# A hybrid decoder layer on one core: the stage of gates, w_out and routing turns its rows by VectorE from quarters of columns instead of by TensorE

## The chip, the core and the metric

The kernel runs on one core of a Trainium2 chip. A core has TensorE (PE: matrix products; PEld is its weight load), VectorE (DVE), ScalarE (ACT), GpSimd (POOL), SyncE (SP, which here only issues transfers) and 16 DMA engines. SBUF has 128 partitions; PSUM takes the products. The metric is the device time of one execution in microseconds, lower is better.

## The reference

One layer over 4096 rows of 1024 float32: adaLN modulation, then a projection that feeds four retention heads and four heads of a gated delta rule, an output projection, and a mixture of 32 experts (4 groups of 8; the best group, then its two best experts). What the changed stage computes is this part:

```python
h = modulate(rmsnorm(x, norm1_w[l]), shift1, scale1)
proj = h @ w_in[l]                 # r_g and d_z are two of its pieces, 512 columns each
ret = rmsnorm(ret).reshape(B, T, RET_WIDTH) * jax.nn.silu(r_g.astype(jnp.float32))
dn = rmsnorm(dn, dn_norm_w[l]).reshape(B, T, DN_WIDTH) * jax.nn.silu(d_z.astype(jnp.float32))
mix = jnp.concatenate([ret, dn], axis=-1).astype(x.dtype) @ w_out[l]
x = x + gate1[:, None, :] * mix
h2 = modulate(rmsnorm(x, norm2_w[l]), shift2, scale2)
# in hierarchical_moe(h2, ...):
group_probs = jax.nn.softmax((xf @ w_group + b_group).astype(jnp.float32), axis=-1)
e_logits = (xf @ w_expert + b_expert).astype(jnp.float32).reshape(n, N_GROUPS, EXPERTS_PER_GROUP)
```

## The kernel before

The kernel has four stages, A (modulation, norm, projections, retention; by blocks of 512 columns), B (convolution and the delta rule, a serial chain of chunks), C (gates, w_out, routing; 32 tiles of 128 rows) and D (experts over slots of rows sorted by expert). Products of float32 accuracy are made of three fp32r products: an operand is split into hi and lo (`split`: ScalarE writes hi, VectorE the difference lo), and `proj` multiplies hi by hi, hi by lo and lo by hi. The code is written out tile by tile; the framework then orders each engine's instructions by a simulated timeline, and tile pools (rooms) set what may overlap. Each engine runs its instructions in order, and so does the issue of transfers on SP.

A tile t of stage C (`c_tile`) goes through these steps. (1) Loads of the normed input in hi and lo (hhC, hlC, two each) and of the retention and delta rows (mix, two); two products pgz of 24 matmuls each; SiLU by ScalarE (sg); the product mix by POOL. (2) TensorE turns mix by eight transposes against the identity (ptm), which are split into mh and ml. (3) Two products poC of 24 matmuls with w_out; VectorE adds x (xC) to each; the sum is stored (acc_d), its squares are summed by ScalarE, the reciprocal root is taken by POOL in small steps (VectorE for the last tile), VectorE scales, POOL adds B2; the rows h2 are stored. (4) TensorE turns h2 by eight transposes (pth); ScalarE copies them to hTC. (5) Eight fp32 products pl with the 36 columns of the router (wr) give logits, VectorE adds the bias (LT), and after each four tiles TensorE turns four LT back (plt) for the routing of that block (`route`; the running ranks come from products prk, and POOL scatters to tab_d).

`phase_c` steps these generators so that the gates of tile t + 1 stand beside w_out of tile t. w_out itself (`wo_block`, two blocks of 512 columns) is loaded on ScalarE's queue, scaled by the modulation's gate (and dn_norm_w for the delta half) and split; the second block is made at the stage's start. Its rooms, like those of xC and hTC, come from one pool of 27 (`wtile`).

## Time and profile before

| | |
|---|---|
| median of 3 runs | 4120.11 us (4109.51 to 4123.87) |
| the profiled execution's own time | 4121.5 us |
| its span | 4119.7 us, mean granted TensorE clock 0.981 |
| TensorE busy | 95% of the span |
| VectorE, ScalarE, POOL busy | 60%, 39%, 37% |
| stage C | about 1715 to 2640 us |

The profile is of one execution. A page gives averages over the whole span; the other views used here are the busy time by stretches, groups of instructions by line, and timelines. "Idle before" names the instruction or transfer that ended the wait. Line numbers are those of the kernel before, except where a row of the kernel after is shown. The granted clock tells what share of full speed the chip gave TensorE. TensorE's instruction lasts longer than the distance to the next one's start, as instructions overlap; distances between starts are used for its pace.

### The profile page before, as it was taken

What the parts mean: (1) busy time and instruction counts of PE and PEld (TensorE: products, weight loads), DVE (VectorE), ACT (ScalarE), POOL (GpSimd) and SP (SyncE); (2) the same over time, 40 slices, a digit from 0 to 9 for tenths busy, and PEclk for the clock granted to TensorE, in tenths of its full rate; (3) what the DMA queues carried; (4) which work ended last, traced back from release to release, by engine and by line L of the source; (5) the groups of instructions that cost most, each with busy time, mean ns of one, the idle gap of its engine ahead of it and who ended that gap; (6) DMA issues with size and microseconds to landing.
All of it is one profiled execution on the core that took longest, in us unless ns stands there. A gap on an engine that the chain in (4) does not pass through costs nothing.

```text
span 4119.7 us, 73091 instructions
## 1 busy us (share of the span) xinstructions
PE 3911.6 (95%) x27074; PEld 3515.6 (85%) x27074; DVE 2467.8 (60%) x6437; ACT 1587.3 (39%) x3298; POOL 1525.5 (37%) x2133
## 2 busy tenths in 40 slices
PE   5999999999999999979999999699999999999997
PEld 4888889899999999968888888598888888888886
DVE  6555543577778777742222222557777777777785
ACT  3433443444544444421122211234444444444453
POOL 2333334234443344222333333433333443454442
PEclk9999999999999999989999999799999999999999
DMA  6443322422222222453333333346666675666673
GB/s 194 137 128 123 98 91 89 115 59 74 58 60 66 74 61 60 118 158 120 118 123 123 123 123 111 119 142 209 204 225 226 216 237 193 232 209 206 225 233 125
DMA packets 459759, 577.48 MB, mean 140 GB/s; under 512 B 97296, under 2 KB 361720, under 8 KB 459400
## 3 DMA queue, kind: packets, MB, share of 16 engines
q1 hardware_dynamic: 411112, 464.72, 36.4%
q0 software_dynamic: 45632, 102.64, 7.4%
q10 hardware_dynamic: 2656, 5.42, 0.4%
q8 instruction: 214, 3.51, 0.4%
q14 instruction: 145, 1.19, 0.1%
HBM read 458.94 MB, written 166.78 MB: 152 GB/s over the span
## 4 chain that ended last, share of the span: by engine, by line
PE 77%; DVE 8%; DMA 8%; issue 3%; ACT 2%; SPq 1%; POOL 1%; DVEq 0%; POOLq 0%; ACTq 0%
PE ph L1410 5%; PE ph L1411 5%; PE ph L1409 5%; PE pjB L523 4%; PE pjB L522 4%; PE pjB L524 4%; PE py L1502 3%; PE py L1503 3%; PE py L1504 3%; PE pgz L291 3%; PE pgz L292 3%; PE pgz L290 3%; PE poC L291 3%; PE poC L292 3%; PE poC L290 3%
## 5 line engine op out<-in xcount | busy, mean ns | idle before, releaser
L1410 PE MATMUL ph<-xl,whD 128*128 128x240 f32 (+7 forms) x2048 | 588.2, 288 | 3.5 <-DVE xl L72 3.2
L1409 PE MATMUL ph<-xh,whD 128*128 128x240 f32 (+7 forms) x2048 | 580.1, 289 | 11.6 <-DVE ssD L1330 6.5
L1411 PE MATMUL ph<-xh,wlD 128*128 128x240 f32 (+7 forms) x2048 | 586.4, 288 | 0.0
L71 ACT ACTIVATE whD<-rawD 128x1024 fp32r<-128x1024 f32 x384 | 400.9, 1056 | 316.0 <-PE py L1503 125.9
L72 DVE TENSOR_TENSOR wlD<-rawD,whD 128x1024 fp32r<-128x1024 f32 x384 | 460.9, 1218 | 35.1 <-ACT whD L71 33.2
L522 PE MATMUL pjB<-hhB,whi 128*128 128x260 f32 x1536 | 443.1, 291 | 9.5 <-DVE cv L530 4.2
L523 PE MATMUL pjB<-hlB,whi 128*128 128x260 f32 x1536 | 440.7, 288 | 6.3 <-DMA hlB<-hl_d 6.1
L524 PE MATMUL pjB<-hhB,wlo 128*128 128x260 f32 x1536 | 440.8, 288 | 0.0
L1409 PEld LDWEIGHTS ph<-xh,whD 128*128 128x128 f32 x2048 | 388.9, 191 | 17.6 <-DVE ssD L1330 7.1
L1410 PEld LDWEIGHTS ph<-xl,whD 128*128 128x128 f32 x2048 | 391.1, 191 | 8.2 <-DVE xl L72 5.3
L1411 PEld LDWEIGHTS ph<-xh,wlD 128*128 128x128 f32 x2048 | 390.9, 191 | 1.9
L522 PEld LDWEIGHTS pjB<-hhB,whi 128*128 128x128 f32 x1536 | 289.0, 189 | 13.9 <-DMA hhB<-hh_d 4.5
L523 PEld LDWEIGHTS pjB<-hlB,whi 128*128 128x128 f32 x1536 | 290.3, 189 | 10.7 <-DMA hlB<-hl_d 8.3
L524 PEld LDWEIGHTS pjB<-hhB,wlo 128*128 128x128 f32 x1536 | 290.1, 189 | 1.6
L532 POOL TENSOR_TENSOR cv<-cv,cv 128x256 f32<-128x256 f32 x192 | 142.0, 740 | 399.2 <-DVE Xd L602 140.5
L1502 PE MATMUL py<-whD,hh 128*128 128x512 f32 (+4 forms) x640 | 259.5, 405 | 12.4 <-DVE hh L69 7.6
L1503 PE MATMUL py<-wlD,hh 128*128 128x512 f32 (+4 forms) x640 | 252.8, 395 | 0.0
L1504 PE MATMUL py<-whD,hl 128*128 128x512 f32 (+4 forms) x640 | 245.9, 399 | 4.6 <-DVE hl L72 4.3
L946 DVE TENSOR_TENSOR xC<-poC,xC 128x512 f32<-128x512 f32 x64 | 44.2, 691 | 329.6 <-PE poC L292 329.6
L1537 POOL DMA_INDIRECT acc_d<-ag,to x80 | 112.2, 1403 | 345.9 <-DVE ag L1510 257.9
L530 DVE SCALAR_TENSOR_TENSOR cv<-pjB,cw,cv 128x256 f32<-128x256 f32 x384 | 183.1, 479 | 78.8 <-ACT cv L528 71.5
L290 PE MATMUL pj<-whi,hh 128*128 128x512 f32 x512 | 205.8, 402 | 6.0 <-ACT whi L71 6.0
(449 smaller groups left out, 10234.4 us busy)
## 6 DMA issues: line engine op xcount, KB each, us to landing
rawD<-in_w_dram SPq DMA_DIRECT2D x384, 512.0 KB
wa<-in_w_ada_dram SPq DMA_DIRECT2D x48, 512.0 KB
hhB<-hh_d SPq DMA_DIRECT2D x64, 260.0 KB
hlB<-hl_d SPq DMA_DIRECT2D x64, 260.0 KB
acc_d<-xC SPq DMA_DIRECT2D x32, 520.0 KB
wraw<-in_w_in_dram SPq DMA_DIRECT2D x32, 512.0 KB
hh_d<-hh SPq DMA_DIRECT2D x16, 1024.0 KB
hl_d<-hl SPq DMA_DIRECT2D x16, 1024.0 KB
```

The costliest lines, as they stand in the source:

```text
L71: nc.scalar.activation(hi, src, AF.Copy)
L72: (e_lo or nc.vector).tensor_tensor(lo, src, hi.bitcast(F32) if hasattr(hi, "bitcast") else hi, op=ALU.subtract)
L290: nc.tensor.matmul(out, a, hi, start=(k == 0), stop=False)
L522: nc.tensor.matmul(pj, wh, hh[k], start=(k == 0), stop=False)
L523: nc.tensor.matmul(pj, wh, hl[k], start=False, stop=False)
L524: nc.tensor.matmul(pj, wl, hh[k], start=False, stop=(k == KD - 1))
L1409: nc.tensor.matmul(ph[nm], hi, xh[:, k, 0:n], start=(k == 0), stop=False)
L1410: nc.tensor.matmul(ph[nm], hi, xl[:, k, 0:n], start=False, stop=False)
L1411: nc.tensor.matmul(ph[nm], lo, xh[:, k, 0:n], start=False, stop=(k == KD - 1))
L1502: nc.tensor.matmul(py[i], a, hi, start=(k == 0), stop=False)
L1503: nc.tensor.matmul(py[i], a, lo, start=False, stop=False)
L1504: nc.tensor.matmul(py[i], b, hi, start=False, stop=(k == 3))
```

## The change

Turning no longer uses TensorE. A new function `turn` reads 128 rows of 1024 back from DRAM in four transfers, one for each quarter of the columns: quarter q goes to partitions 32q to 32q + 31, with the four groups of 32 rows side by side. Two VectorE instructions then transpose all blocks of 32x32 in it. The result has features on the partitions in another order of features than before, so w_out, dn_norm_w (dnw) and the router's weights are loaded in that order, in four transfers each per block.

For the mixed rows this means a new DRAM tensor mg_d, written in two halves; for h2 its store, which was there, is read back. Both use one room seg and one pair tr; xC and h2 also have one room each, kept for the whole stage. The splits of the mixed rows read tr instead of PSUM. hT now has hi and lo side by side, and the router's weights hi and lo as 72 columns, so that eight fp32r products of 256 columns replace eight fp32 ones of 128; LT is added from both halves, and one product a tile with a fixed matrix sel gives the logits by rows. The reciprocal root and the addition of B2 move from POOL to VectorE. The generators are stepped so that the gates of a tile stand up to three tiles ahead of its w_out product, and only tile 0's gates stand in front of the stage's set-up.

```diff
...
-            eng.dma_start(raw[:, :, 0:512], src[rows].rearrange("(a p) n -> p a n", p=P))
+            if seg:
+                for q in range(4):
+                    r = 256 * q + 64 * k2
+                    eng.dma_start(raw[32 * q:32 * q + 32, :, 0:512], src[r:r + 64].rearrange("(a i) n -> i a n", i=32))
+            else:
+                eng.dma_start(raw[:, :, 0:512], src[rows].rearrange("(a p) n -> p a n", p=P))
...
+            self.tr = [self.xp.tile([P, 4, P + 2], F32, name="tr", tag="h", bufs=10)[:, :, 0:P] for _ in range(2)]
             tile_(0)
             self.wo.append(self.wo_block(1, p))
+            self.seg, self.xw, self.h2 = (self.wtile(nm, F32) for nm in ("seg", "xC", "h2C"))
+            next(run[0])
+            next(run[0])
+            tile_(1)
...
+            wr = p.tile([P, KD, 36], F32, name="wr", tag="hT", bufs=1)
+            for q in range(4):
+                w = wr[32 * q:32 * q + 32]
+                for c, src in ((slice(0, 4), self.w_group), (slice(4, 36), self.w_expert)):
+                    nc.sync.dma_start(w[:, :, c], src[0][256 * q:256 * q + 256].rearrange("(k i) n -> i k n", i=32))
+            self.wr = p.tile([P, KD, 72], F32R, name="wr2", bufs=1)
+            self.split(self.wr[:, :, 0:36], self.wr[:, :, 36:72], wr)
+            self.br = br = p.tile([72, 1], F32, name="brt", bufs=1)
...
+            self.sel = p.tile([72, 36], F32, name="sel", bufs=1)
+            nc.vector.tensor_tensor(self.sel, self.ident[0:72, 0:36], self.ident[0:72, 36:72], op=ALU.add)
...
             for t in range(NT + 1):
+                if t + 2 < NT:
+                    tile_(t + 2)
                 if t + 1 < NT:
-                    tile_(t + 1)
-                if t < NT:
-                    next(run[t])
-                if t >= 1:
-                    next(run[t - 1])
+                    next(run[t + 1])
                 if late:
                     next(late, None)
                     late = None
+                if t < NT:
+                    next(run[t])
+                if t + 1 < NT:
+                    next(run[t + 1])
                 if t < NT:
                     next(run[t])
...
         def scale(raw, k2):
-            g = g1[:, None].to_broadcast([P, 2, 512])
-            if k2 < 2:
-                nc.vector.tensor_tensor(raw, raw, g, op=ALU.mult)
-            else:
-                nc.vector.scalar_tensor_tensor(raw, raw, self.dnw, g, op0=ALU.mult, op1=ALU.mult)
...
+            for a in range(2):
+                k = 2 * k2 + a
+                nc.vector.scalar_tensor_tensor(raw[:, a], raw[:, a], self.dnw[:, k:k + 1], g1, op0=ALU.mult, op1=ALU.mult)
+
+        return self.wblock(self.w_out[0][:, 512 * i:512 * i + 512], nc.scalar, scale=scale, pool=pool, seg=True)
...
-        mix = []
         for i, d in enumerate((self.ret_d, self.dn_d)):
-            mix.append(self.xp.tile([P, 512], F32, name="mix", tag=f"x{i}", bufs=2))
-            nc.sync.dma_start(mix[i], d[rows, :])
-        for i in range(2):
+            mix = self.xp.tile([P, 512], F32, name="mix", tag=f"x{i}", bufs=2)
+            nc.sync.dma_start(mix, d[rows, :])
             pg = self.psum([P, 512], "pgz", "pj")
             sg = self.xp.tile([P, 512], F32, name="sg", bufs=1)
             self.proj(pg, *hs, 0, self.gz[i], 0, 512)
             nc.scalar.activation(sg, pg, AF.Silu)
-            nc.gpsimd.tensor_tensor(mix[i], mix[i], sg, op=ALU.mult)
-        xw = self.wtile("xC", F32)
-        x = xw[:, 0:D]
-        nc.gpsimd.memset(xw[:, D:], 0.0)
-        nc.sync.dma_start(x, self.x[0, rows, :])
+            nc.gpsimd.tensor_tensor(mix, mix, sg, op=ALU.mult)
+            nc.sync.dma_start(self.mg_d[rows, 512 * i:512 * i + 512], mix)
         yield
-
-        if t < 2:
+        self.turn(self.mg_d[rows])
+        yield
+
+        if t == 0:
             mh, ml = ([self.xp.tile([P, 4, P + 2], F32R, name=n, tag="h", bufs=10)[:, :, 0:P] for _ in range(2)]
                       for n in ("mhx", "mlx"))
         else:
             mh, ml = (p.tile([P, KD, P], F32R, name=n, bufs=1).rearrange("p (i k) n -> i p k n", i=2)
                       for n in ("mh", "ml"))
         for i in range(2):
-            pt = self.psum([P, 4, P], "ptm", "tp")
-            for a in range(4):
-                nc.tensor.transpose(pt[:, a], mix[i][:, a * P:(a + 1) * P], self.ident)
-            self.split(mh[i], ml[i], pt)
+            self.split(mh[i], ml[i], self.tr[i])
+        xw = self.xw
+        x = xw[:, 0:D]
+        nc.gpsimd.memset(xw[:, D:], 0.0)
+        nc.sync.dma_start(x, self.x[0, rows, :])
...
-        h2 = p.tile([P, D], F32, name="h2", bufs=2)
+        h2 = self.h2[:, 0:D]
         nc.scalar.activation(h2, x, AF.Square, accum_out=ss)
         nc.vector.tensor_scalar(ss, ss, 1.0 / D, EPS, op0=ALU.mult, op1=ALU.add)
-        last = t == self.NT - 1
-        self.rsqrt_b(p, ss, ss, 1, None if last else nc.gpsimd)
-        if last:
-            for i in range(2):
-                c = slice(512 * i, 512 * i + 512)
-                nc.vector.scalar_tensor_tensor(h2[:, c], x[:, c], ss, self.A2[:, c], op0=ALU.mult, op1=ALU.mult)
-                nc.vector.tensor_tensor(h2[:, c], h2[:, c], self.B2[:, c], op=ALU.add)
-        else:
-            nc.vector.scalar_tensor_tensor(h2, x, ss, self.A2, op0=ALU.mult, op1=ALU.mult)
-            nc.gpsimd.tensor_tensor(h2, h2, self.B2, op=ALU.add)
+        self.rsqrt_b(p, ss, ss, 1)
+        nc.vector.scalar_tensor_tensor(h2, x, ss, self.A2, op0=ALU.mult, op1=ALU.mult)
+        nc.vector.tensor_tensor(h2, h2, self.B2, op=ALU.add)
         nc.sync.dma_start(self.h2_d[rows, :], h2)
...
-        hT = self.wtile("hTC", F32)[:, 0:D].rearrange("p (k n) -> p k n", k=KD)
+        hT = p.tile([P, KD, 2, P], F32R, name="hT", bufs=1)
+        self.turn(self.h2_d[rows])
         for i in range(2):
-            pt = self.psum([P, 4, P], "pth", "tp")
-            for a in range(4):
-                nc.tensor.transpose(pt[:, a], h2[:, (4 * i + a) * P:(4 * i + a + 1) * P], self.ident)
-            nc.scalar.activation(hT[:, 4 * i:4 * i + 4], pt, AF.Copy)
+            k = slice(4 * i, 4 * i + 4)
+            self.split(hT[:, k, 0], hT[:, k, 1], self.tr[i])
         yield
         q, j = self.block_of[t]
         n = len(self.blocks[q])
         if j == 0:
             LG[q] = p.tile([P, 4, 36], F32, name="LG", bufs=1)[:, :n]
-            LT[q] = p.tile([36, 4, P], F32, name="LT", bufs=1)
-        LG, LT = LG[q], LT[q]
-        pl = self.psum([36, P], "pl", "lv")
+
+        pl = self.psum([72, 2, P], "pl", "lv")
         for k in range(KD):
             nc.tensor.matmul(pl, self.wr[:, k], hT[:, k], start=(k == 0), stop=(k == KD - 1))
-        nc.vector.tensor_scalar(LT[:, j], pl, self.br, None, op0=ALU.add)
-        if j == n - 1:
-            pt = self.psum([P, 4, 36], "plt", "tp")
-            for i in range(n):
-                nc.tensor.transpose(pt[:, i], LT[:, i], self.ident[0:36, 0:36])
-            nc.vector.tensor_copy(LG, pt[:, :n])
+        LT = p.tile([72, P], F32, name="LT", bufs=1)
+        nc.vector.tensor_scalar(LT, pl[:, 0], self.br, None, op0=ALU.add)
+        nc.vector.tensor_tensor(LT, pl[:, 1], LT, op=ALU.add)
+        pt = self.psum([P, 36], "plt", "tp")
+        nc.tensor.matmul(pt, LT, self.sel, start=True, stop=True)
+        nc.vector.tensor_copy(LG[q][:, j], pt)
...
+    def turn(self, src):
+
+        nc = self.nc
+        seg = self.seg[:, 0:D]
+        for q in range(4):
+            nc.sync.dma_start(seg[32 * q:32 * q + 32].rearrange("j (b c) -> j b c", b=4),
+                              src[:, 256 * q:256 * q + 256].rearrange("(b j) c -> j b c", b=4))
+        for a in range(2):
+            nc.vector.transpose(self.tr[a].rearrange("p k (b j) -> p b k j", b=4),
+                                seg.rearrange("p (b k i) -> p b k i", b=4, k=KD)[:, :, 4 * a:4 * a + 4])
...
```

How the order moves is shown at three places. The first is VectorE in the steady stage, around the scaling of one tile's rows (h_24190 before, h2C after; A_ is A2, B_ is B2). Before:

```order
L946 TENSOR_TENSOR xC<-poC,xC 128x512 x2
L951 TENSOR_SCALAR ssC<-ssC 128x1
L431 TENSOR_SCALAR rb_y<-ssC 128x1
L980 TENSOR_SCALAR LT<-pl,brt 36x128
L432 TENSOR_SCALAR rb_y<-rb_y 128x1
L960 SCALAR_TENSOR_TENSOR h_24190<-xC,ssC,A_21058 128x1024
L72 TENSOR_TENSOR ml<-ptm,mh 128x512 x2
L946 TENSOR_TENSOR xC<-poC,xC 128x512 x2
```

And after, from the end of the reciprocal root on; the first two rows of tr are the turn of this tile's h2, the second two that of the mixed rows two tiles on:

```order
L445 SCALAR_TENSOR_TENSOR ssC<-rb_t,rb_y 128x1
L974 SCALAR_TENSOR_TENSOR h2C<-xC,ssC,A_21185 128x1024
L975 TENSOR_TENSOR h2C<-h2C,B_21186 128x1024
L997 COPY LG<-plt 128x36
L1007 STREAM_TRANSPOSE tr<-seg 128x4x4x32 x2
L72 TENSOR_TENSOR hT<-tr,hT 128x4x128 x2
L967 TENSOR_TENSOR xC<-poC,xC 128x512
L1007 STREAM_TRANSPOSE tr<-seg 128x4x4x32 x2
L967 TENSOR_TENSOR xC<-poC,xC 128x512
L72 TENSOR_TENSOR ml<-tr,mh 128x512
```

Four transposes, two splits and the addition of B2 stand in VectorE's order where none stood, and one pair of transposes stands between the two additions of the next tile.

The second place is SyncE's issues in the steady stage, around the store of one tile's normed rows (its DRAM tensor h2_d is printed as h_d). Before:

```order
L947 DMA acc_d<-xC 128x1040
L927 DMA xC<-in_x_dram 128x1024
L911 DMA hlC<-hl_d 128x4x128 x2
L911 DMA hhC<-hh_d 128x4x128 x2
L917 DMA mix<-ret_d 128x512
L917 DMA mix<-dn_d 128x512
L962 DMA h_d<-h_24378 128x1024
```

After:

```order
L968 DMA acc_d<-xC 128x1040
L961 DMA xC<-in_x_dram 128x1024
L976 DMA h_d<-h2C 128x1024
L945 DMA mg_d<-mix 128x512
L934 DMA hhC<-hh_d 128x4x128 x2
L1004 DMA seg<-h_d 32x4x256 x4
L934 DMA hlC<-hl_d 128x4x128 x2
L939 DMA mix<-ret_d 128x512
L945 DMA mg_d<-mix 128x512
L1004 DMA seg<-mg_d 32x4x256 x4
L939 DMA mix<-dn_d 128x512
```

Nine issues a tile are now nineteen; the loads of seg stand behind a tile's hhC and in front of its hlC.

The third place is ScalarE at the start of the stage, where w_out's second half is split (whi) and the mixed rows of tile 0 are split for its first product (mhx). Before:

```order
L89 DMA wraw<-in_w_out_dram 128x2x512
L922 ACTIVATE sg<-pgz 128x512
L71 ACTIVATE mhx<-ptm 128x4x128 x2
L71 ACTIVATE whi<-wraw 128x2x512
L89 DMA wraw<-in_w_out_dram 128x2x512
L71 ACTIVATE whi<-wraw 128x2x512
L71 ACTIVATE mhx<-ptm 128x4x128
L683 ACTIVATE X<-px 32x8x32
```

After:

```order
L757 ACTIVATE o<-pqs,eg 128x128 x4
L93 DMA wraw<-in_w_out_dram 32x2x512 x2
L766 ACTIVATE jk,msB<-o 128x128 x4
L71 ACTIVATE whi<-wraw 128x2x512 x3
L93 DMA wraw<-in_w_out_dram 32x2x512 x4
L71 ACTIVATE whi<-wraw 128x2x512
L71 ACTIVATE mhx<-tr 128x4x128 x2
L71 ACTIVATE wr_21201<-wr 128x8x36
```

Before, mhx stood ahead of the delta rule's last chunks (px and o belong to it); now it stands behind them and behind the last split of w_out.

## Rows read from the trace of the kernel before

**Rows 1.** The page: its first part (busy us, share of the span, instructions of each engine) and the first line of its fourth (the chain of work that ended last, share of the span by engine).

```profile
PE 3911.6 (95%) x27074; PEld 3515.6 (85%) x27074; DVE 2467.8 (60%) x6437; ACT 1587.3 (39%) x3298; POOL 1525.5 (37%) x2133
...
PE 77%; DVE 8%; DMA 8%; issue 3%; ACT 2%; SPq 1%; POOL 1%; DVEq 0%; POOLq 0%; ACTq 0%
```

**Rows 2.** Busy time by stretch of the span. Columns: from:to and length in us; for each engine busy us and (instructions), TensorE first, then its weight loads (PEld), VectorE, ScalarE, POOL; the granted TensorE clock (1.00 is full), the DMA engines' busy share and GB/s.

```profile
1750.00:1800.00 50.00, 39.49 (x251) 32.12 (x250) 23.50 (x45) 14.72 (x32) 15.35 (x23) 0.76 0.43 124
1800.00:1850.00 50.00, 38.52 (x169) 30.33 (x169) 23.26 (x53) 11.38 (x29) 7.85 (x31) 0.90 0.65 198
1850.00:1950.00 100.00, 100.00 (x513) 81.39 (x512) 27.52 (x80) 19.04 (x34) 28.39 (x58) 1.00 0.39 122
2450.00:2550.00 100.00, 100.00 (x508) 81.16 (x507) 28.75 (x88) 19.82 (x35) 38.09 (x76) 1.00 0.38 122
```

**Rows 3.** TensorE's timeline over one tile of stage C and the end of the tile three further on (the fourth from the first). Columns: start in us, duration in us, engine, line, operation, out<-in, shape, count. The last row of the w_out product of a tile is the one with ml in front of pgz.

```profile
2295.92 0.39 PE L292 MATMUL poC<-whi,ml 128*128 128x512 f32 x1
...
2296.38 0.40 PE L290 MATMUL pgz<-whi,hhC 128*128 128x512 f32 x1
2296.71 1.94 PE L979 MATMUL pl<-hTC,wr 128*36 128x128 f32 x16
...
2298.91 0.40 PE L292 MATMUL pgz<-whi,hlC 128*128 128x512 f32 x1
...
2304.46 0.40 PE L292 MATMUL pgz<-whi,hlC 128*128 128x512 f32 x1
...
2305.81 0.39 PE L291 MATMUL pgz<-wlo,hhC 128*128 128x512 f32 x1
...
2311.83 0.40 PE L292 MATMUL poC<-whi,ml 128*128 128x512 f32 x1
2312.07 1.04 PE L968 MATMUL pth<-K,h 128*128 128x128 f32 x8
...
2313.18 0.40 PE L291 MATMUL poC<-wlo,mh 128*128 128x512 f32 x1
...
2401.49 0.39 PE L292 MATMUL poC<-whi,ml 128*128 128x512 f32 x1
```

**Rows 4.** Groups of instructions between 1850 and 2550 us. Columns: line, engine, operation, out<-in, shapes, count | busy us, mean ns of one | idle time before them and what ended it.

```profile
L923 POOL TENSOR_TENSOR mix<-mix,sg 128x512 f32<-128x512 f32 x54 | 70.0, 1297 | 14.3 <-ACT sg L922 13.3
...
L72 DVE TENSOR_TENSOR ml<-ptm,mh 128x512 fp32r<-128x512 f32 x54 | 35.1, 683 | 60.0 <-ACT mh L71 59.9
L960 DVE SCALAR_TENSOR_TENSOR h<-xC,ssC,A 128x1024 f32<-128x1024 f32 x27 | 34.6, 1283 | 80.3 <-POOL ssC L441 80.3
...
L984 PE MATMUL plt<-K,LT 36*128 36x36 f32 x24 | 3.7, 238 | 0.0
```

**Rows 5.** TensorE's timeline in the stage of experts: products of 256 columns, one after another.

```profile
2680.11 0.28 PE L1409 MATMUL ph<-xh,whD 128*128 128x256 f32 x1
2680.22 0.28 PE L1410 MATMUL ph<-xl,whD 128*128 128x256 f32 x1
```

**Rows 6.** VectorE's timeline in the delta rule: a transpose in blocks of 32x32.

```profile
1694.72 0.43 DVE L674 STREAM_TRANSPOSE Tb<-Vb 32x256 f32<-32x256 f32 x1 [2.25 <-DMA Vb<-dgi]
```

**Rows 7.** SyncE's issues beside the tile of rows 3, and under them the DMA engines' busy tenths and GB/s between 2296 and 2312 us in 40 slices of 0.4 us; the first burst in them is the store of xC to acc_d, issued before the load.

```profile
2298.71 0.33 SPq L927 DMA_DIRECT2D xC<-in_x_dram  x1
...
DMA  0000399809869520094999606499998999983200
GB/s 0 0 0 0 146 426 406 354 0 113 225 246 399 236 92 0 0 81 77 294 341 347 169 3 100 111 314 319 338 346 291 328 394 446 394 338 143 92 21 0
```

**Rows 8.** SyncE's issues of small or partitioned transfers, and on VectorE and ScalarE the instruction that waited for one; in square brackets the idle time before it and what ended it.

```profile
1692.97 1.82 SPq L666 DMA_DIRECT2D Vb<-dgi  x4
...
1708.28 1.71 SPq L594 DMA_DIRECT2D L<-dgo  x4
...
1716.34 0.19 DVE L600 TENSOR_TENSOR Ltmp<-Xd,L 128x31 f32<-128x31 f32 x1 [4.29 <-DMA L<-dgo]
...
1815.90 0.92 SPq L763 DMA_DIRECT2D dn_d<-o  x2
...
1818.79 2.00 ACT L71 ACTIVATE whi<-wraw 128x1024 fp32r<-128x1024 f32 x2 [6.57 <-DMA dn_d<-o]
```

**Rows 9.** VectorE's and POOL's timeline at a routing block.

```profile
2357.59 2.39 DVE L994 TENSOR_TENSOR ohg<-ohg,pr 128x16 f32<-128x16 f32 x1
...
2357.55 2.40 POOL L961 TENSOR_TENSOR h<-h,B 128x1024 f32<-128x1024 f32 x1 [1.56 <-DVE ohg L993]
```

**Rows 10.** TensorE's timeline at the start of the w_out products, and VectorE's of the row A2 (named A there).

```profile
1806.67 0.50 PE L290 MATMUL poC<-whi,mhx 128*128 128x512 f32 x1
...
1819.90 1.22 PE L290 MATMUL poC<-whi,mhx 128*128 128x512 f32 x2 [7.41 <-ACT whi L71]
...
1843.48 0.40 PE L292 MATMUL poC<-whi,mlx 128*128 128x512 f32 x1
...
1826.71 1.23 DVE L829 SCALAR_TENSOR_TENSOR A<-A,n 128x1024 f32<-128x1024 f32 x1 [4.48 <-DMA n<-in_norm_w_dram]
```

**Rows 11.** VectorE's timeline at the stage's end, after the last w_out product.

```profile
2625.06 0.69 DVE L946 TENSOR_TENSOR xC<-poC,xC 128x512 f32<-128x512 f32 x1 [1.27 <-PE poC L292]
...
2629.77 0.16 DVE L438 SCALAR_TENSOR_TENSOR ssC<-rb_t,rb_y 128x1 f32<-128x1 f32 x1
...
2638.65 0.20 DVE L985 COPY LG<-plt 128x36 f32<-128x36 f32 x1
```

More of the change, by code (lines that the diff above doesn't have):

```diff
@@ L80, in wtile, with wblock @@
         return (pool or self.wp).tile([P, 1040], dt, name=name, tag="w", bufs=8 if pool else 27)
-    def wblock(self, src, eng, n=512, extra=None, scale=None, pool=None):
+    def wblock(self, src, eng, n=512, extra=None, scale=None, pool=None, seg=False):
         out = []
@@ L109, in setup @@
         self.dn_d = dp.tile([T, 512], F32, name="dn_d")
+        self.mg_d = dp.tile([T, D], F32, name="mg_d")
         self.h2_d = dp.tile([T, D], F32, name="h2_d")
@@ L467, in next_weights @@
                     yield
-                self.dnw = self.xp.tile([P, 1], F32, name="dnw", bufs=1)
-                nc.sync.dma_start(self.dnw, self.dn_norm_w.rearrange("o p -> p o"))
+                self.dnw = self.xp.tile([P, KD], F32, name="dnw", bufs=1)
+                nc.vector.memset(self.dnw, 1.0)
+                for q in (2, 3):
+                    for a in range(2):
+                        nc.sync.dma_start(self.dnw[32 * q:32 * q + 32, 4 * a:4 * a + 4],
+                                          self.dn_norm_w.rearrange("o (k i) -> i (o k)", i=32))
                 self.wo = [self.wo_block(0)]
@@ L809, in phase_c @@
         tc, nc, T = self.tc, self.nc, self.T
-        with tc.tile_pool(name="C", bufs=2) as p:
-            LG, LT, run = {}, {}, []
+        with tc.tile_pool(name="C", bufs=2, reuse_waits="tile") as p:
+            LG, run = {}, []
             def tile_(t):
-                run.append(self.c_tile(p, t, LG, LT))
+                run.append(self.c_tile(p, t, LG))
                 next(run[t])
@@ L894, in scale, with c_tile @@
         def scale(raw, k2):
[L895 to L903 removed]
+            for a in range(2):
+                k = 2 * k2 + a
+                nc.vector.scalar_tensor_tensor(raw[:, a], raw[:, a], self.dnw[:, k:k + 1], g1, op0=ALU.mult, op1=ALU.mult)
+        return self.wblock(self.w_out[0][:, 512 * i:512 * i + 512], nc.scalar, scale=scale, pool=pool, seg=True)
+    def c_tile(self, p, t, LG):
         nc = self.nc
```

11 lines of the change are left out of this document (3 added, 8 removed).

## The prediction, made before the changed kernel ran

> **What bounds the kernel now.** I read the page first: TensorE is busy 95% of the span and is 77% of the chain that ended last, VectorE 8%, DMA 8% [rows 1]. That is an average over stages, so I went to the busy time by stage [rows 2]: from 1850 to 2550 us, seven stretches of which the first and the last stand there, TensorE works 100 of every 100 us at the full granted clock (2.4 GHz), VectorE 28 and 29, ScalarE 19 and 20, POOL 28 and 38. So in the middle of the changed stage only TensorE's instruction time counts. At its start the picture differs: 39.49 of 50 us (clock 0.76) and 38.52 of 50 (0.90).
>
> Then one tile in TensorE's timeline [rows 3]: the last w_out matmul of a tile starts at 2295.92, that of the fourth tile on at 2401.49, so a tile takes 105.57/4 = 26.39 us. The 96 matmuls of 512 columns start 0.2316 us apart: 22.2 us. The rest is inserted work, each priced as the gap less two spacings: the logits pl 2298.91 − 2296.38 − 0.46 = 2.07; the transposes ptm 2305.81 − 2304.46 − 0.46 = 0.89; pth 2313.18 − 2311.83 − 0.46 = 0.89.
>
> **The change, part by part, in the steady stage.**
> *Removed from TensorE:* ptm and pth, 1.78 us a tile.
> *Logits:* eight fp32 matmuls of 128 columns (sixteen passes) become eight fp32r ones of 256. Those of 256 columns in the stage of experts start 0.12 us apart [rows 5]: 8 × 0.12 = 0.96, a gain of 1.1. If the 72 columns of hi and lo cost nothing extra this stands; the bound above is 2.07, no gain.
> *plt* is now one matmul a tile with 128 rows out instead of four in a row after four tiles: 0.24 us busy each [rows 4], about 0.1 more a tile; bounds 0 and 0.4.
> *Sum:* 26.39 − 1.78 − 1.1 + 0.1 = **23.6 us a tile**, 2.8 less (1.7 to 2.9).
>
> *Where the work goes.* A turned row tile is now stored to DRAM, read back in four DMAs of 32 partitions, transposed by two VectorE instructions and split. The trace has a 32x256 stream transpose of 0.43 us [rows 6]; 128x512 has twice the columns, so I take 0.87 (bounds 0.6, a subtraction of that width from PSUM being 0.69 [rows 4], and 1.3), 3.5 us a tile for four. VectorE also gets two splits, the rsqrt chain and the + B2 from POOL: some 8 us more beside 7 us now; busy share is no bound.
>
> *The loop.* There is one room seg and one pair tr, and VectorE runs in order. VectorE's rows of after, shown with the change, give the cycle: the transposes of the normed tile, then the transposes of the mixed tile two on, which stand ahead of the second addition of the next w_out tile, from which the next normed tile comes. Its length, from that addition:
> addition to the squares' sum 2.0 (it starts at 2625.06, the rsqrt chain ends at 2629.77, 4.7 in all with 14 small steps [rows 11]; I take 4.9); scaling 1.28 [rows 4]; + B2 1.28 by the same width; so the store is issued at 7.6.
> Store S: two stores of 256 KB were issued from 1815.90 and had released ScalarE at 1818.79 [rows 8]: 2.8.
> Load Q, four quarters: the 512 KB of xC are issued at 2298.71; the DMA slices of 0.4 us run again from 2299.6 and fall off after 2302.0 [rows 7]: 3.3. Four issues take 1.71 instead of 0.3 [rows 8], but the first three overlap the data; I take 3.7. Bounds: 1.75 (Vb, four loads of 32 KB, issued at 1692.97, used at 1694.72 [rows 6, 8]) and 8.1 (tile L of the delta rule, four loads of the same sort, issued at 1708.28 behind a 512 KB load, used at 1716.34 [rows 8]).
> Loop = 7.6 + 2.8 + 3.7 + 1.74 + 3.7 + 1.74 = **21.3 us**, under 23.6. I stay near the row of xC because it moves as many bytes at the same place; the DMA engines' share is 0.38 there [rows 2], and a tile moves some 4.5 MB instead of 3.0.
> The logits have six more us of room (hT is ready about 17 us after the w_out tile; they stand at 23). SP's queue: the loads of hhC and hlC stand between; their waits for gate matmuls are for 36 and 48 gate matmuls, 9.7 and 12.5 us after the tile's end with the logits, and seg's first load is due at 10.4 anyway.
>
> *One more price on that loop.* A VectorE instruction of 16 columns took 2.39 us, started with POOL's 2.40 us addition and ended with it [rows 9]. POOL loses that addition. It keeps two multiplications of 1.30 a tile [rows 4]. The rows show no instruction of 512 columns held so. The Trainium skill, "SBUF — State Buffer", section "SBUF: two separate sides", says that a VectorE instruction with two SBUF inputs and a GpSimd one take a port pair in turns, each for its whole length; the splits now read SBUF, not PSUM, and by that rule up to 2.6 us a tile go into the loop, 23.9 in place of 21.3. I leave the sum at 21.3 and hold the 2.6 for the rivals.
>
> **Start of the stage.** Before, gates of three tiles (148 gate matmuls) filled the idle time of the delta-rule chain, w_out began at 1806.67 with waits for w_out's second half (7.41 us for ScalarE's split), and the second tile's last matmul is at 1843.48 [rows 10]. After, only one tile's gates lie there (48). ScalarE's rows show that the w_out tile 0 now waits behind all splits of w_out's second half, whose last raw block comes behind A2 (at 1826.71 before [rows 10]). The chain may end some 6 us earlier without gates in its way (px), so A2 at about 1820, then scaling 2 × 0.69, transposes 1.74, splits 1.06 + 0.6: w_out begins at **1823** (1812 to 1835). Then 240 matmuls × 0.2316 = 55.6 and about 3 us at the lower clock (1.2 GHz, as in the stretch of 0.76): tile 1 ends at 1882, against 1843.7 with 44 gate matmuls (10.2 us) fewer still to do. Loss: 38 − 10 = **28 us** (15 to 40). Sixteen DMA issues a block instead of four are in ScalarE's queue, some 5 us, within that range.
>
> **From there to the last tile.** 2784 matmuls × 0.2316 = 645; 30 tiles' logits and the rest, 23.6 − 22.2 = 1.4 each, 42; and at the end, where no gates are left to cover the last turn, 11 (Q, transposes and splits 7, the rest lower clock): 698. The last w_out tile ends at 2580, before at 2625.06 [rows 11].
>
> **Tail.** Before, from there to the last logits 2638.65 − 2625.06 = 13.6 [rows 11], on which a serial chain to the experts hangs. After: 7.0 to the store, 2.8, 3.7, 1.74, splits 1.7, logits at the low clock 1.9, rest 1.1: 20. Loss **6.4** (4 to 12).
>
> **Sum**, against the profiled run's own 4121.5 us (span 4119.7; the median 4120.1 is 1.4 lower): last logits at 2600 instead of 2638.65, so 38.5 less: **4083 us**. Stages A, B and experts keep their order; the small DMAs for dnw, wr and br hide beside the matmuls of B and the wait for A2.
>
> **Rivals.**
> 1. *The loop is a little longer than TensorE's 23.6* (Q near 5, or Q 3.7 with the 2.6 of POOL's multiplications and slow hops): 25 us a tile. Then 29 tiles × 1.4 = 40 are given back: about 4123. For it: 50% more bytes, and bursts that share queues with hhC, hlC and mix. Against it: xC's slices. It decides from Q = 4.9 on (21.3 + 2 × 1.2 = 23.7).
> 2. *The loop is the bound outright, slower than before:* with Q = 6.5 it is 26.9, TensorE idles 3.3 us a tile, 29 × 3.3 = 96 are lost: 4179. It crosses the old pace of 26.39 at Q = 6.25. The row at 8.1 speaks for it, that it stood behind other loads against it. The Trainium skill, "VectorE: DVE Perf Modes", section "The three transpose paths", sends a full 128x128 transpose to TensorE, since VectorE's spans only 32x32 blocks; moving the blocks is then a DMA's work, which is this loop.
> 3. *The start is worse:* w_out begins at 1840 and the pipeline stays dry for a tile, some 20 more: 4103.
> 4. *The start is better,* w_out at 1808: 4068.
>
> **How the numbers follow.** The forecast 0.45; start better 0.12; start worse 0.10; loop at about 25 us 0.18; loop over 26 us 0.15. The range must leave out no more than 2 in 10: from 4060 to 4145 it leaves the outright loop (0.15) and a little of the best. The forecast's own range is 4070 to 4100. A change of 0.3% (12 us) is about what a measurement here can tell from none. Faster than that: the forecast, both starts but a part of the worse, and a part of the mild loop: 0.66. Same: 0.14. Slower: 0.20.
>
> **What would show it.** TensorE's row from 1900 to 2500: 100 of 100 with tiles 23.6 us apart says the loop is hidden; a repeated wait of w_out on ScalarE's or VectorE's mh or ml split with VectorE idle on seg says it is not. Seg's issue to the transpose's start gives Q; the transposes' mean gives 0.87. w_out's first matmul gives the start; the stretch from the last w_out matmul to the last logits gives the tail. Wrong is the prediction if tiles are further apart than 24 us, or if the stage begins after 1840.

## The result, and the profile of the kernel after

The changed kernel takes 4160.41 us (median of 4 runs, 4153.26 to 4169.65), the kernel before beside it 4117.42: a ratio of 1.0107, with a 95% interval of 1.0078 to 1.0135. It is 1.1% slower; 4083 and "faster" were forecast, with 4060 to 4145 as the range. The profiled execution has a span of 4161.2 us.

The page of the kernel after, the two lines that answer to [rows 1]:

```profile
PE 3848.0 (92%) x26338; PEld 3449.4 (83%) x26338; DVE 2677.1 (64%) x7034; ACT 1593.3 (38%) x3299; POOL 1365.6 (33%) x1699
...
PE 59%; DMA 16%; DVE 13%; issue 5%; ACT 3%; SPq 3%; POOL 1%; DVEq 0%; ACTq 0%; POOLq 0%
```

TensorE is busy for 64 us less (3848.0 against 3911.6), and yet the time grew. The chain that ended last tells where to look: TensorE's share fell from 77 to 59%, DMA's doubled to 16%, VectorE's rose from 8 to 13%. Busy time by stretch of the kernel after (columns as in [rows 2]) places it:

```profile
1750.00:1800.00 50.00, 20.77 (x184) 18.86 (x184) 30.62 (x73) 15.62 (x38) 7.66 (x16) 0.60 0.33 94
1800.00:1850.00 50.00, 31.24 (x125) 25.09 (x126) 13.41 (x19) 5.64 (x9) 2.70 (x3) 0.77 0.68 183
2200.00:2300.00 100.00, 93.70 (x419) 74.24 (x419) 52.25 (x151) 20.29 (x34) 18.85 (x20) 0.98 0.63 177
2400.00:2500.00 100.00, 90.41 (x407) 71.27 (x406) 49.13 (x137) 20.05 (x34) 18.16 (x20) 0.98 0.65 177
```

In the steady stage TensorE is no longer busy 100 of 100 us but 90 to 94. (Its instructions there number 407 to 419 in 100 us where the kernel before had some 510; that alone says little, as a tile now has some 23 fewer of them, 736 over the 32 tiles.) No other engine is full either, nor are the DMA engines (VectorE about 51%, DMA 65%). When nothing is full, a chain of waits is the first thing to look for. The last w_out matmul of a tile comes 26.55 us after that of the tile in front, against 26.36 before and 23.6 forecast. (Here and below, the distance of tiles is a mean over 16 of them, four routing blocks, from the starts of these matmuls: 2144.02 to 2568.84 us in the kernel after, 2111.11 to 2532.92 before.) One turn of that chain, in the timelines of VectorE, SyncE and POOL in the kernel after:

```profile
2205.75 0.69 DVE L967 TENSOR_TENSOR xC<-poC,xC 128x512 f32<-128x512 f32 x1
...
2212.88 0.32 SPq L976 DMA_DIRECT2D h_d<-h2C  x1
2213.30 0.38 SPq L934 DMA_DIRECT2D hhC<-hh_d  x1
...
2215.33 0.96 POOL L1112 DMA_INDIRECT tab_d<-dat,si  x1 [0.30 <-issue]
...
2216.36 1.30 POOL L944 TENSOR_TENSOR mix<-mix,sg 128x512 f32<-128x512 f32 x1
...
2217.69 0.32 SPq L945 DMA_DIRECT2D mg_d<-mix  x1
2218.10 0.39 SPq L934 DMA_DIRECT2D hhC<-hh_d  x1
2218.58 1.93 SPq L1004 DMA_DIRECT2D seg<-h_d  x4
...
2224.05 1.31 DVE L1007 STREAM_TRANSPOSE tr<-seg 128x512 f32<-128x512 f32 x2 [11.10 <-DMA seg<-h_d]
...
2225.39 1.74 SPq L1004 DMA_DIRECT2D seg<-mg_d  x4
...
2230.80 1.31 DVE L1007 STREAM_TRANSPOSE tr<-seg 128x512 f32<-128x512 f32 x2 [3.44 <-DMA seg<-mg_d]
2232.03 0.65 DVE L967 TENSOR_TENSOR xC<-poC,xC 128x512 f32<-128x512 f32 x1
```

From addition to addition: 7.13 to the store of h2, 5.70 until SyncE issues the first quarter, 5.47 until the transposes, 1.34 to the next first quarter, 5.41 to its transposes, 1.23 to the addition: 26.28. VectorE stands still 11.10 and then 3.44 us for the two loads. Ahead of the first quarter SyncE's queue held the store of a half of mg_d and a load of hhC until 2217.69 and 2218.10. That half was late because this tile is one with routing: POOL issued eight scatters to tab_d, the last at 2215.33, and its product mix stands behind them. In five of the 25 tiles of the table below, all of them with routing, the step to the first quarter is 5.7 us for this reason; the median of all is 3.9. The means of these steps over 25 tiles between 1900 and 2600 us, worked out from VectorE's and SyncE's timelines, beside what the prediction took:

| step of the chain | forecast | after, mean of 25 |
|---|---|---|
| second addition to the store of h2 | 7.6 | 7.86 |
| store to the first quarter's issue | 2.8 | 4.46 |
| first quarter's issue to the transposes, h2 | 3.7 | 6.44 |
| transposes to the next first quarter | 1.74 | 1.33 |
| first quarter's issue to the transposes, mixed rows | 3.7 | 4.94 |
| transposes to the second addition | 1.74 | 1.54 |
| sum | 21.3 | 26.6 |

TensorE's own wait at the end of the tile after it, for hT (its timeline):

```profile
2252.80 1.20 PE L991 MATMUL pl<-hT,wr 128*72 128x256 f32 x8 [1.68 <-DVE hT L72]
```

The view of the tile seg, between 1900 and 2600 us, gives who waits for it and how long a quarter is under way:

```profile
its engine sat idle before it (us, times) until:
  DMA seg<-h_d: 235.4, 27
  DMA seg<-mg_d: 77.7, 27
...
DMA to landing us min/median/max: 2.5/3.8/6.2
```

235.4 / 27 = 8.7 us a tile of VectorE's idle time ended with h2's quarters, 2.9 with the mixed rows'.

The start and the end of the stage in the kernel after: the first w_out product; the second tile's last one; the last tile's second addition; its logits.

```profile
1818.76 0.80 PE L297 MATMUL poC<-whi,mhx 128*128 128x512 f32 x1 [26.28 <-ACT mhx L71]
...
1876.55 0.40 PE L299 MATMUL poC<-whi,ml 128*128 128x512 f32 x1
...
2665.38 0.68 DVE L967 TENSOR_TENSOR xC<-poC,xC 128x512 f32<-128x512 f32 x1
...
2685.11 0.20 DVE L997 COPY LG<-plt 128x36 f32<-128x36 f32 x1 [0.74 <-PE plt L996]
```

With [rows 10, 11]: the second tile ends 33.1 us later, with 10.2 us of gates more done: 22.9 lost. From there to the last tile's second addition it takes 788.8 us now and 781.6 before; so the 1.8 us of transposes a tile and the cheaper logits bring nothing back. From that addition to the last logits it takes 19.7 us against 13.6.

### The profile page after: what moved, and what is told of

Same layout as the page of the kernel before. It is cut to its first block, busy times and chain, and to the rows that moved or that the text cites. A ratio compares the mean times of both kernels' runs of the same rounds, so it can differ in the third digit from the quotient of the medians.

```text
span 4161.2 us, 72221 instructions
## 1 busy us (share of the span) xinstructions
PE 3848.0 (92%) x26338; PEld 3449.4 (83%) x26338; DVE 2677.1 (64%) x7034; ACT 1593.3 (38%) x3299; POOL 1365.6 (33%) x1699
## 3 DMA queue, kind: packets, MB, share of 16 engines
q14 instruction: 150, 1.23, 0.1%
## 4 chain that ended last, share of the span: by engine, by line
PE 59%; DMA 16%; DVE 13%; issue 5%; ACT 3%; SPq 3%; POOL 1%; DVEq 0%; ACTq 0%; POOLq 0%
PE ph L1433 5%; PE ph L1434 5%; PE ph L1432 5%; PE pjB L533 4%; PE pjB L534 4%; PE pjB L535 4%; DMA seg<-h_d 3%; PE py L1525 3%; PE py L1526 3%; PE py L1527 3%; PE pj L297 3%; PE pj L298 3%; DMA seg<-mg_d 3%; PE pj L299 3%; DVE wlD L72 2%
## 5 line engine op out<-in xcount | busy, mean ns | idle before, releaser
L1007 DVE STREAM_TRANSPOSE tr<-seg 128x512 f32<-128x512 f32 x128 | 83.6, 692 | 343.5 <-DMA seg<-h_d 247.9
```

## The experiments

The theories: **A**, the one room seg and VectorE's order put the two turns of each tile in series, and that chain, longer than TensorE's 23.6 us, sets the pace; with it **A1** (the four issues of 32 partitions and 1 KB pieces make the loads long) and **A2** (other transfers in flight do). **B**, the DMA engines or TensorE set the pace, and the chain only follows.

**Two rooms.** The turn of h2 reads its quarters back into h2's own room; seg belongs to the mixed rows.

```diff
-    def turn(self, src):
+    def turn(self, src, room=None):
...
-        seg = self.seg[:, 0:D]
+        seg = (self.seg if room is None else room)[:, 0:D]
...
-        self.turn(self.h2_d[rows])
+        self.turn(self.h2_d[rows], self.h2)
```

> The turn of the normed rows reads back into the room of h2 itself (free once the rows are stored), so seg belongs to the mixed rows alone; all else is the changed kernel. In its profile a tile of the steady stage takes 26.6 us, and the mean steps of the cycle store, first quarter of h2, transposes, first quarter of the mixed rows, transposes, second addition, store are 4.5 + 6.4 + 1.3 + 4.9 + 1.5 + 7.9 us. Theory A (the one room strings the two turns in series, and that chain is longer than TensorE's work): the 4.9 and one 1.3 leave the chain, which becomes about 20.4 to 21.7 us, TensorE is the bound at 23.6 us a tile, and the kernel is 27 x 3.0 = 80 us faster than the changed one: about 4080 us. Theory B (the DMA engines, 65% busy in the stage, can move no more than a tile in 26.6 us): the quarters land as late as before, the tile stays at 26 to 27 us, and the time within 15 us of 4160.

Measured: 4061.14 us, 0.9881 of the kernel before (0.9859 to 0.9903). Tiles are 23.56 us apart. Busy time by stretch, and one tile in the timelines of VectorE and SyncE:

```profile
2200.00:2300.00 100.00, 100.00 (x469) 81.74 (x468) 57.41 (x172) 23.76 (x40) 18.80 (x20) 1.00 0.68 197
...
2202.22 1.75 SPq L1004 DMA_DIRECT2D seg<-mg_d  x4
...
2214.75 1.75 SPq L1004 DMA_DIRECT2D h2C<-h_d  x4
...
2222.18 1.31 DVE L1007 STREAM_TRANSPOSE tr<-h2C 128x512 f32<-128x512 f32 x2 [10.94 <-DMA h2C<-h_d]
2224.80 0.70 DVE L1007 STREAM_TRANSPOSE tr<-seg 128x512 f32<-128x512 f32 x1
```

The quarters of the mixed rows are now issued 12.5 us ahead of those of h2, and their transposes follow h2's with no wait. (The framework moved orders with it: one transpose of the mixed rows now stands on either side of the first addition.) TensorE is back at 100 of 100 us and moves on at the forecast's 23.6 us. The load of h2 is as long as before (2214.75 to 2222.18, mean 6.31 over 27 tiles), and the DMA engines carry more than in the kernel after (0.68, 197 GB/s against 0.63, 177): B falls, A holds. The same row says that the price of TensorE's part was right.

**Transposes twice,** with one room and with two.

```diff
-        for a in range(2):
+        for a in (0, 1, 0, 1):
             nc.vector.transpose(self.tr[a].rearrange("p k (b j) -> p b k j", b=4),
```

> Each turn does its two VectorE transposes twice, with the same result; all else is the changed kernel. VectorE is 51% busy there, so its sum is no bound. Theory A (the chain through seg sets the pace): 2 x 1.31 = 2.6 us more for each tile, 26.6 becomes 29.2, the kernel about 2.6 x 28 = 73 us slower than the changed one, about 4233 us. Theory B (DMA throughput or TensorE sets it): VectorE waits for the quarters anyhow, and the time is within 15 us of 4160.

> Two rooms, with the two VectorE transposes of each turn done twice (5.2 us of VectorE a tile instead of 2.6). With one room the same doubling cost 1.0 us a tile (26.66 to 27.64), with VectorE's order changed too (the second addition moved in front of the mixed rows' transposes). Theory A: with two rooms TensorE is the bound and the chain is 2 to 3 us shorter than its 23.6, so the doubling is covered: tiles of 23.6 to 24.0 us, the time within 12 us of 4061. If VectorE's own work or the DMA engines set the 23.6, tiles of 24.6 us or more, some 30 us slower.

Measured with one room, in a single run: 4182.62 us, tiles of 27.57 us, 1.0 more and not the 2.6 expected. The framework had reordered VectorE by its simulated timeline: in most tiles the second addition moved in front of the mixed rows' transposes. One tile in the timelines of VectorE and SyncE, from store to store:

```profile
2303.05 0.32 SPq L976 DMA_DIRECT2D h_d<-h2C  x1
...
2313.45 1.30 DVE L1007 STREAM_TRANSPOSE tr<-seg 128x512 f32<-128x512 f32 x2 [3.98 <-DMA seg<-h_d]
2314.93 1.30 DVE L1007 STREAM_TRANSPOSE tr<-seg 128x512 f32<-128x512 f32 x2
2316.94 0.68 DVE L967 TENSOR_TENSOR xC<-poC,xC 128x512 f32<-128x512 f32 x1
2320.66 1.30 DVE L1007 STREAM_TRANSPOSE tr<-seg 128x512 f32<-128x512 f32 x2 [1.19 <-DMA seg<-mg_d]
...
2330.85 0.45 SPq L976 DMA_DIRECT2D h_d<-h2C  x1
```

Both loads are still on the chain, 27.8 us from store to store here: the mixed rows' transposes now stand between the second addition and the scaling. What left it are that addition and the sum of squares, which run while the mixed rows are under way. So the run changed two things, and the 2.6 can't be read from it. With two rooms, also in a single run: 4098.5 us, tiles of 24.55, where 23.6 to 24.0 was expected. That expectation took the chain as 20.4 to 21.7 us, which is too short. In the run with two rooms (means of 25 tiles) its steps are 7.2 (addition to store), 4.3 (store to first quarter), 6.5 (load) and 5.0 (transposes to the second addition, without the 0.5 us a tile for which VectorE waits there for w_out's product): 23.0, some 0.5 us under TensorE's 23.6. In the doubled run (24 tiles) they are 7.5, 3.9, 6.2 and 7.0, together 24.6, and that wait is gone: the chain has become the bound, and its sum is the distance of tiles.

**One plain load instead of four quarters.**

```diff
-        for q in range(4):
-            nc.sync.dma_start(seg[32 * q:32 * q + 32].rearrange("j (b c) -> j b c", b=4),
-                              src[:, 256 * q:256 * q + 256].rearrange("(b j) c -> j b c", b=4))
+        nc.sync.dma_start(seg, src)
```

> The changed kernel, but each turn reads its 128 rows by one transfer of 128 partitions with 4 KB each instead of four quarters of 32 partitions with pieces of 1 KB; so the turned rows are not those of the reference (the sorting of column quarters to partitions is left out), the rest of the work is the same, with VectorE's and SyncE's order as changed. It prices the shape of the load on the chain of seg (in the changed kernel's profile 6.4 and 4.9 us from the first quarter's issue to the transposes). Theory A1 (the four issues and small pieces make the load long): both loads fall to the 3.3 to 3.7 us that the prediction took, the chain to 22 us, TensorE bounds at 23.6 a tile, about 4080 us. Theory A2 (the other transfers in flight make it long): only the three issues of some 0.45 us go, loads of 5.0 and 3.6, chain and tile near 24 us, about 4090 us.

**Without the gates' loads** (from tile 8 on).

```diff
+        if t >= 8:
+            hs = self.hs8
         for d, nm in ((self.hh_d, "hhC"), (self.hl_d, "hlC")):
+            if t >= 8:
+                break
...
+        self.hs8 = hs
```

> The changed kernel, but from tile 8 on the gates use the hhC and hlC of tile 7 (the loads of their own normed input are left out: 1 MB less a tile; the products are all done); order of VectorE as changed. Theory A2 (the loads of hhC and hlC, issued just ahead of and behind the quarters of h2, make them long): from the first quarter to the transposes 4.2 us instead of 6.4 for h2 and 4 instead of 4.9 for the mixed rows, and the store's step 3.8 instead of 4.5 without SyncE's waits for the gate products: chain 22.8, tile 23.6 us, about 4095 us (24 tiles of 3.0 less). Theory A1 (shape of the load): 6.4 and 4.9 stay, only the store's step shortens: tile 25.9 us, about 4143 us.

The whole times, 4521.06 and 4288.5 us, each of a single run, missed both expectations and say nothing: the rows that the router sees are other ones, they go to other experts, and the time from the last logits to the end is 1933 and 1656 us instead of 1476. Read in stage C alone, one tile with the plain load and then one without the gates' loads, SyncE's and VectorE's timelines:

```profile
2210.35 0.33 SPq L1003 DMA_DIRECT2D seg<-h_d  x1
...
2215.78 1.31 DVE L1005 STREAM_TRANSPOSE tr<-seg 128x512 f32<-128x512 f32 x2 [8.92 <-DMA seg<-h_d]
...
2217.11 0.33 SPq L1003 DMA_DIRECT2D seg<-mg_d  x1
...
2220.48 1.31 DVE L1005 STREAM_TRANSPOSE tr<-seg 128x512 f32<-128x512 f32 x2 [1.39 <-DMA seg<-mg_d]
```

```profile
2215.67 1.74 SPq L1009 DMA_DIRECT2D seg<-h_d  x4
...
2220.00 1.30 DVE L1012 STREAM_TRANSPOSE tr<-seg 128x512 f32<-128x512 f32 x2 [7.74 <-DMA seg<-h_d]
...
2221.33 1.74 SPq L1009 DMA_DIRECT2D seg<-mg_d  x4
...
2225.90 1.31 DVE L1012 STREAM_TRANSPOSE tr<-seg 128x512 f32<-128x512 f32 x2 [2.59 <-DMA seg<-mg_d]
```

The means over 28 tiles each, beside the kernel after:

| | load of h2 | load of mixed rows | store to first quarter | tile |
|---|---|---|---|---|
| after | 6.44 | 4.94 | 4.46 | 26.55 |
| one plain load | 4.98 | 3.74 | 4.14 | 23.53 |
| no gates' loads | 4.76 | 4.68 | 4.20 | 24.56 |

On the chain VectorE's order is that of the kernel after in both. The plain load takes 1.5 and 1.2 us off. That is about three issues of 0.42 us; the run changes the number of issues and the shape of the pieces together, so that the issues are the cause is likely, not shown. Leaving out the gates' loads, issued around h2's quarters, takes 1.7 us off h2's load and 0.3 off the mixed rows'. The tiles at the end of the stage, where no gates are left to load, show the same without any change to the loads: h2's quarters take 4.3 to 4.4 us in the last five tiles with two rooms, and the plain load 3.4 to 3.7 in the last three of its run, 5.2 on average ahead of them. So neither theory had it alone: of h2's 6.4 us some 3.5 are the plain load by itself, 0.8 to 1.5 come with the four quarters and 1.6 to 2.1 with the neighbours; the mixed rows' 4.9 are their plain load's 3.7 and 1.2. Either gain brings the tile down by 2 or 3 us, so both runs speak for A as the two rooms do.

**Quarters from ScalarE's queue.**

```diff
-            nc.sync.dma_start(seg[32 * q:32 * q + 32].rearrange("j (b c) -> j b c", b=4),
+            nc.scalar.dma_start(seg[32 * q:32 * q + 32].rearrange("j (b c) -> j b c", b=4),
```

> The changed kernel, but the quarters are issued from ScalarE's queue instead of SyncE's, so they stand behind no hhC, mix or mg_d issue on SyncE. ScalarE then waits in order for each store to land. Theory A2 (what is queued on the same queue makes the loads long): 4 to 4.5 us for each, tile 24 us, about 4090 us, unless ScalarE's waits push sg or the squares back. Theory A1 (shape, or the engines shared by all queues): within 0.7 us of 6.4 and 4.9 each, tile 26 us or more, 4145 to 4200 us.

Measured, in a single run: 4195.47 us, tiles of 27.81 us. ScalarE's and VectorE's timelines:

```profile
2227.09 2.03 ACTq L1004 DMA_DIRECT2D seg<-h_d  x4
...
2234.43 1.31 DVE L1007 STREAM_TRANSPOSE tr<-seg 128x512 f32<-128x512 f32 x2 [11.70 <-DMA seg<-h_d]
...
2235.78 1.76 ACTq L1004 DMA_DIRECT2D seg<-mg_d  x4
...
2241.66 1.31 DVE L1007 STREAM_TRANSPOSE tr<-seg 128x512 f32<-128x512 f32 x2 [4.16 <-DMA seg<-mg_d]
```

In this tile the loads take 7.3 and 5.9 us, and 7.7 and 5.6 as means of 25 tiles, longer than from SyncE; the place in SyncE's queue is not what made them long. That the neighbours take their share on the DMA engines, whichever queue issues, is the likely reading; no run shows where. VectorE's order differs in a few rows here, so only the loads are read, not the total.

**The parts by themselves.** The first of these has h2 turned by VectorE and the mixed rows by TensorE; the second has both turns on TensorE with the router in parts. The core of the edit against the kernel after, for the first and then for the second on top of it (w_out's loads and the stepping of tiles are those of before, and mg_d is not written):

```diff
-        self.turn(self.mg_d[rows])
-        yield
...
-            self.split(mh[i], ml[i], self.tr[i])
+            pt = self.psum([P, 4, P], "ptm", "tp")
+            for a in range(4):
+                nc.tensor.transpose(pt[:, a], mix[i][:, a * P:(a + 1) * P], self.ident)
+            self.split(mh[i], ml[i], pt)
...
-        self.turn(self.h2_d[rows])
...
-            self.split(hT[:, k, 0], hT[:, k, 1], self.tr[i])
+            pt = self.psum([P, 4, P], "pth", "tp")
+            for a in range(4):
+                nc.tensor.transpose(pt[:, a], h2[:, (4 * i + a) * P:(4 * i + a + 1) * P], self.ident)
+            self.split(hT[:, k, 0], hT[:, k, 1], pt)
```

> Half of the change: the normed rows are turned by VectorE from quarters, with the router in parts and the root and B2 on VectorE as changed; the mixed rows are turned by TensorE as before, w_out loads and the stepping of the tiles (gates one tile on) are those of before. One turn a tile means no second load on the chain. Theory A: store to logits is 4.5 + 6.4 + 1.3 + 1.4 + 7.9 = 21.5 us after a tile's end, under the distance of about 24.5 to the logits' place; a tile is TensorE's 26.39 - 0.89 (pth) - 1.1 (logits) + 0.1 = 24.5 us; the start of the stage is that of before; 31 x 1.9 = 59 less and some 6 more at the tail: about 4065 us. Theory B (every turn through DRAM costs its waits on TensorE): TensorE waits for hT each tile, tiles of 26 us or more, 4110 or slower.

> No turning by VectorE at all: both turns on TensorE and the stepping of before, with the router in parts (eight fp32r products of 256 columns, 72 columns of weights, one product for the rows a tile) and the root and B2 on VectorE. It prices that part alone. By the prediction's terms a tile goes from 26.39 to 26.39 - 1.1 + 0.1 = 25.4 us: about 31 us less than before, 4087 us. If the products of 256 columns with 72 columns of weights cost what the sixteen passes did, nothing changes (within 10 us of before).

Measured: h2 only 4074.68 us, 0.9913 of before (0.9896 to 0.9930), tiles of 24.44 (24.5 expected; the whole was expected at 4065, and what the other 10 us are stays open). Router only 4086.75 us, 0.9939 of before (0.9916 to 0.9961), tiles of 25.30 (25.4 expected). Busy time of 2200 to 2300 us in the first and in the second:

```profile
2200.00:2300.00 100.00, 100.00 (x481) 81.77 (x480) 53.85 (x162) 21.55 (x36) 19.92 (x22) 1.00 0.48 148
```

```profile
2200.00:2300.00 100.00, 100.00 (x498) 82.11 (x497) 46.78 (x146) 20.48 (x36) 19.07 (x20) 1.00 0.40 126
```

One turn a tile through DRAM leaves TensorE at 100 of 100: it is not the way through DRAM that costs, but two of them in series.

**Gates earlier.** Two rooms, and the gates of tile 1 (then of tiles 1 and 2) written ahead of the set-up of w_out's second half; the second edit is shown.

```diff
             tile_(0)
+            tile_(1)
+            tile_(2)
             self.wo.append(self.wo_block(1, p))
...
             next(run[0])
             next(run[0])
-            tile_(1)
...
-                if t + 2 < NT:
+                if 1 <= t and t + 2 < NT:
                     tile_(t + 2)
```

> The kernel with two rooms (h2's quarters read back into h2's own room), with the gates of tile 1 written ahead of the set-up of w_out's second half, so that 95 instead of 48 gate products lie in the tail of the delta rule, where TensorE stood idle for 22 us ahead of the first w_out product. If that idle time is free for them, about 47 x 0.23 = 11 us less, part of it given back where the last products of the delta rule wait behind gates (px): 4050 us, against 4061 for two rooms alone. If the delta rule's chain is delayed by as much, no difference (4061).

> Two rooms as before (h2's quarters go back into h2's room), with the gates of tiles 1 and 2 written ahead of the set-up of w_out's second half: 143 gate products lie in the tail of the delta rule, as many as in the kernel before, instead of 48 (two rooms alone) or 95 (early gates of one tile, 4053.9 us). If TensorE is still idle there, another 48 x 0.23 = 11 us less, some given back to the delta rule's chain: 4045 us. If the first w_out product moves back by as much, because the chain's products wait behind gates, 4054 or more.

Measured: 4053.86 us, 0.9853 of before (0.9824 to 0.9882), and 4046.50 us, 0.9841 (0.9815 to 0.9866). The two intervals overlap; that the second is the faster is likely, not shown. In the second, TensorE works 37.58 of 50 us between 1750 and 1800 instead of 21.23 with two rooms alone:

```profile
1750.00:1800.00 50.00, 37.58 (x256) 32.04 (x254) 27.33 (x54) 17.30 (x45) 14.72 (x24) 0.80 0.50 143
```

The first w_out product begins later, at 1820.41 (1814.81 with two rooms alone), but 96 more gate products are done by then, and the second tile ends at 1856.05 instead of 1872.70. It is the fastest kernel of this study, 1.6% under the one before.

## Why the prediction was wrong, point by point

*TensorE's part* was right. The tile price of 23.6 us was measured three times where TensorE worked 100 of 100 us: 23.56 with two rooms, 23.53 with the plain load, 23.54 with early gates. So were its terms: the router part 26.36 − 25.30 = 1.06 us where 1.0 net was taken, the normed rows' transposes 25.30 − 24.44 = 0.86 and the mixed rows' 24.44 − 23.56 = 0.88, where 0.89 was taken for each.

*The loop* is the step that failed, and it failed by its size, not by its shape. The prediction found the chain, wrote its steps in the right order and put it at 21.3 us; it is 26.6 (the mean of the 25 tiles of the table). Three quarters of the miss of 5.3 is the term Q, the load of four quarters: 3.7 was taken for each, 6.4 and 4.9 were measured. The row that it was read from, xC, is a single transfer with little beside it; as a single plain transfer the mixed rows do take 3.7. What that row could not show is that four quarters take 0.8 to 1.5 us more than one load, though the first three issues were held to overlap the data, and that hhC and hlC are under way at the same time because the change's own order puts them around the quarters. The share of the DMA engines, 0.38 on average, was used as an argument against this; an average says nothing of what is in flight at the moment that the chain waits.

Another 1.7 us is the term S: the store's quarters could follow after 2.8 by the row of two stores of 256 KB (2.9 by its own times); the median is 3.9. The store itself takes 3.6 to 5.2 us from issue to landing (median 3.8), and in the tiles with routing the quarters wait for the half of mg_d behind POOL's scatters, which makes the mean 4.46. The prediction had dismissed the waits in SyncE's queue as over before. The transposes, 0.69 us each instead of 0.87, gave 0.6 back.

That both terms grow with what is beside them shows at the last tile, where SyncE issues nothing else (SyncE's and VectorE's rows of the kernel after):

```profile
2672.45 0.34 SPq L976 DMA_DIRECT2D h_d<-h2C  x1
...
2675.12 1.74 SPq L1004 DMA_DIRECT2D seg<-h_d  x4
...
2679.45 1.31 DVE L1007 STREAM_TRANSPOSE tr<-seg 128x512 f32<-128x512 f32 x2 [3.14 <-DMA seg<-h_d]
```

There S is 2.7 and Q 4.3 us.

*POOL's hold on VectorE* was left out of the sum and turned up. A step of one element a partition took 1.14 us beside POOL's multiplication, in the kernel after (VectorE's row, then POOL's):

```profile
2235.78 1.14 DVE L445 SCALAR_TENSOR_TENSOR rb_y<-rb_t,rb_y 128x1 f32<-128x1 f32 x1
...
2235.59 1.31 POOL L944 TENSOR_TENSOR mix<-mix,sg 128x512 f32<-128x512 f32 x1
```

Both end at 2236.9. Steps of this kind take 0.16 us elsewhere in the chain. The Trainium skill, "SBUF — State Buffer", section "SBUF: two separate sides", has such pairs exclude each other for a whole instruction, and the trace agrees, with 1.0 us in most tiles (8.1 from addition to store, 7.1 in the routing tiles, where POOL scatters instead): 20 steps of one element a partition between 1900 and 2600 us took 1.13 to 1.30. Up to 2.6 a tile had been held for it. Without it the step from addition to store is 7.1, so the 7.6 of the sum was 0.5 too much, and the mean of 7.86 hides both.

*The rivals.* The second one came true: the loop as the bound outright, slower than before, at 26.9 us a tile and 4179; measured were 26.55 and 4160. Its chance was set at 0.15. The threshold was stated for Q alone (6.25); with S 1.7 longer as well, the measured mean Q of 5.7 was enough. The rows that spoke for a long load (8.1 behind another load) were there and were put aside for the nearest in size.

*The start* was right: first product at 1818.76 (1823 forecast), second tile's end at 1876.55 (1882), loss 22.9 (28, in the range). Its cause was right too: that product waited 26.28 us for ScalarE's split mhx. *The tail* was right: 19.7 us (20), a loss of 6.1 (6.4). *From the second tile to the last*, 788.8 us in place of 698 is 91 more. Less the 5 us by which the start was better, the last logits come 85 us later than forecast, at 2685.11 instead of 2600. The profiled execution (4163.1 us) misses the 4083 by 80, as the time from there to the end is 5 us shorter than before, which was not followed up; the median misses it by 77.

## What to carry to other kernels

A new path off the busy engine must be priced as a loop: every room that it uses once a turn and every engine that runs it in order closes one, and its length stands against the busy engine's period; here 26.6 us against 23.6 turned 2.8 us a tile of saved work into a loss, and a second room, which was free at that moment anyway, gave it all back. Price a transfer on such a loop by its own issues and by what the new order puts in flight beside it, not by a lone transfer of the same size and an average share. And where a stage's inputs decide the work of a later one, read an experiment that falsifies them by its stage and not by its total.

## What the runs showed of the hardware that was not expected

A transpose of 128x512 in 32x32 blocks took 0.69 us (0.67 to 0.72), no longer than a subtraction of that size, where 0.87 was scaled from 32x256. Four quarters that together carry 512 KB took 1.2 to 1.5 us longer from the first issue to use than one transfer of 512 KB (0.8 us in the last tiles, with no gates' loads beside them), near the time of the three further issues; the gates' loads around them cost 1.6 to 2.1 us more. Moved to another queue, the loads did not get shorter (7.3 and 5.9 us in the tile shown). A store of 512 KB to DRAM took 3.6 to 5.2 us from issue to landing in the steady stage.
